# Second-half operand sums pinned over gate/up units 4 to 14, the last chunk's norm moved into unit 2, and the down stage's pools laid elsewhere

## The chip, the cores and the metric

The kernel runs on one core of a Trainium2 chip. The metric is device time in microseconds for one execution of the whole program; lower is better. The core has five engines with queues of their own that run in order: TensorE (PE), VectorE (DVE), ScalarE (ACT), GpSimd (POOL) and SyncE (SP), which here issues nearly all of the loads and stores. An instruction at the head of a queue that waits for a semaphore holds everything behind it on that queue.

## The reference

One transformer block on 2048 tokens of width 1024: three kinds of self-attention, a projection, cross-attention over 256 memory tokens, and a gated feed-forward layer. The change touches the seam between the cross-attention and the feed-forward layer, the feed-forward layer's first half, and the start of its down projection:

```python
def _rmsnorm(x, g):
    y = xf * lax.rsqrt(jnp.mean(xf * xf, axis=-1, keepdims=True) + EPS)
    return y * g
...
x = x + _cross(_rmsnorm(x, norm_cross), _rmsnorm(mem, norm_mem), w_cq, w_ckv, w_co)
h = _rmsnorm(x, norm_ffn)
gate, up = jnp.split(h @ w_gu, 2, axis=-1)          # 1024 -> 2 x 2816
x = x + (jax.nn.silu(gate) * up) @ w_down           # 2816 -> 1024
return _rmsnorm(x, final_norm)
```

## The kernel before, in words

All is fp32; each matmul operand is split into a rounded high part (`h`, a cast on ACT) and the rest (`l`, a subtraction on DVE or POOL), and a product is three matmuls (`mm3`, L87 to L95). Tokens lie in four chunks of 512 columns. A scheduler puts the instructions of each engine into an order of its own from the program's order and from the pools' tiles; an instruction that is given to `tc.keep_in_program_order` keeps its program place among those so pinned on its engine. Tiles of one tag share `bufs` buffers, and a new tile waits for the last use of the one that it replaces.

**Cross-attention** runs 16 units `u` (four heads for each chunk). `soft` (L1057) makes the probabilities `cp` of a unit, normalised by `l` at L1074; `turn_p` transposes them on PE (L1082); `outp` (L1098 to L1106) multiplies by `w_co`, adds the residual and adds squares into `ssum` on POOL (L919). `rows` (L1108 to L1115) transposes a chunk's result back to row order for a store. `norm1` and `norm2` (L1117 to L1134) give the feed-forward norm of a chunk: column sums on PE (`rc`, L925), a reciprocal root on ACT and DVE, a diagonal `dg`, a broadcast matmul, a copy `rb`, and eight scalings (L1132), whose results go to DRAM as `s_h3`. Chunks 0 and 1 form the first half of the feed-forward stage, chunks 2 and 3 the second.

**Gate and up** run two halves of 22 units `f`. A unit is a Strassen-like step: seven products p1, p5, p2, p6, p7, p3, p4 in this order, each 12 matmuls of 128x512, so 84 matmuls. The token-side operands of a half are "11", "t1", "21", "t2", "t3", "22", "t4", with four parts each; `turn1` (L1165 to L1168) splits a part, with part 3's low half on POOL and the others on DVE. The weight-side operands come from `prep_w(f)` (L1292 on): two loads `graw` (three buffers), sums s1 to s4 on DVE (L1304 to L1307), and seven splits `awh`, `awl` (L1239, L1240; four buffers; products 0, 3 and 6 on DVE, the rest on POOL). A unit's results are added on DVE, ACT and POOL and stored as `s_g` (L1372, L1382).

**The second half's sums.** `second(j)`, called before units 3, 7, 11 and 15, makes the operands of the second half from `s_h3` of chunks 2 and 3: four loads, three casts on ACT (L1257), three splits (L1258) and four subtractions (L1263 to L1268) on POOL, and nine stores to `s_b`. `refill` (L1272) loads them back near the first half's end. Nothing in it is pinned in this kernel.

**Down** (L1427 on) runs groups of two hidden blocks `js`, the first group of one. `weights` loads `draw` from `w_down` and makes sums; `tokens` loads `graw` from `s_g`; `parts` splits either (cast L1441, low part L1443) into `wdh`, `wdl`, `gdh`, `gdl`; the matmuls are at L1547. All of its pools lie on the left of the SBUF, the raw loads `draw` first, over the tiles of the gate and up stage that its last unit still stores from.

Of the kernel before, what the change touches and what calls it, by code (L numbers as in the profile page):

```python
# [33 lines left out]
def kernel(ctx: ExitStack, tc: tile.TileContext, a: dict, out: bass.AP, dbg=None):  # L34
# [9 lines left out]
    def scratch(shape, name):  # L44
        if name in dbg:
# [15 lines left out]
    s_x2 = [[scratch([P, CH], f"s_x2_{c}_{k}") for k in range(KT)] for c in range(NCH)]  # L61
    s_x3 = [scratch([CH, D], f"s_x3_{c}") for c in range(NCH)]
    s_b = {n: [[scratch([P, CH], f"s_b{n}_{j}_{i}") for i in range(2 if n in ("11", "t1", "21") else 1)]
               for j in range(4)] for n in ("11", "t1", "21", "t2", "t3", "t4")}
    s_h3 = [[scratch([P, CH], f"s_h3_{c}_{k}") for k in range(KT)] for c in range(NCH)]
# [855 lines left out]
    def rms_cols(st):  # L921

        ps = pp.tile([P, CH], F32, name="rc", tag="tp", bufs=2)
        for t in range(4):
            nc.tensor.matmul(ps[:, t:t + 1], st[0][:, t * P:(t + 1) * P], ones[:, 0:1], start=True, stop=True)  # L925
# [131 lines left out]
    def soft(u, q):  # L1057
# [15 lines left out]
        for t in range(4):  # L1073
            nc.vector.tensor_scalar_mul(pt[:, t, :], pt[:, t, :], l[:, t:t + 1])  # L1074
        return pt
# [62 lines left out]
    def load_wc(k):  # L1138
        th, tl = wp.tile([P, D], F32R, name=f"wch{k}"), wp.tile([P, D], F32R, name=f"wcl{k}")
        for n in range(2):  # L1140
            r = lp.tile([P, CH], F32, name="wraw", tag="x3", bufs=9)
            nc.sync.dma_start(r, a["w_co"][0][k * P:(k + 1) * P, n * 512:(n + 1) * 512])
            split(r, th[:, n * 512:(n + 1) * 512], tl[:, n * 512:(n + 1) * 512])
        wc.append((th, tl))
# [88 lines left out]
    with ExitStack() as es:  # L1233
# [11 lines left out]
        def turn(B, n, raw):  # L1245
            for j in range(4):
                turn1(B, n, j, raw[j])

        def second(j):

            b11, b21, b12, b22 = (pools["fx"].tile([P, CH], F32, name="ht", tag="ht", bufs=16) for _ in range(4))
            for x, y in zip((b11, b21, b12, b22), (s_h3[2][j], s_h3[2][4 + j], s_h3[3][j], s_h3[3][4 + j])):
                nc.sync.dma_start(x, y)

            def parts(n, x):
                t = [pools["fx"].tile([P, CH], F32, name="ht", tag="ht", bufs=16) for _ in range(2)]
                nc.scalar.copy(t[0].bitcast(F32R), x)  # L1257
                nc.gpsimd.tensor_sub(t[1].bitcast(F32R), x, t[0])  # L1258
                for i in range(2):
                    nc.sync.dma_start(s_b[n][j][i], t[i])  # L1260

            parts("11", b11)
            nc.gpsimd.tensor_sub(b11, b12, b11)  # L1263
            parts("t1", b11)
            nc.gpsimd.tensor_sub(b12, b22, b12)
            nc.gpsimd.tensor_sub(b11, b22, b11)
            parts("21", b21)
            nc.gpsimd.tensor_sub(b21, b21, b11)  # L1268
            for n, x in (("t2", b11), ("t3", b12), ("t4", b21)):
                nc.sync.dma_start(s_b[n][j][0], x)  # L1270

        def refill():  # L1272
# [126 lines left out]
        xlate.close()  # L1399
# [225 lines left out]
```

## Time and profile before

| | |
|---|---|
| three runs | 2868.70, 2869.55, 2871.01 us; median 2869.55 |
| the profiled execution | 2869.44 us, of which the span is 2867.7 |
| PE busy | 2734.8 us, 95% of the span |
| DVE, ACT, POOL busy | 1865.8 (65%), 1316.5 (46%), 1356.4 (47%) |
| DMA | 409.76 MB, mean 143 GB/s |

The span is what the profiler saw from the first to the last instruction. PE's share is so high that shares alone say little; what counts are the stretches in which PE stands still or runs at the lower of its two clock levels. PEclk in a view of stretches is the clock granted as a share of the full 2.4 GHz; 0.5 is 1.2 GHz. A wait is put down to the instruction that released it.

### The profile page before, as it was taken

How to read it: one execution, taken by the hardware profiler on the slowest of the kernel's cores; microseconds unless marked ns; L12 is line 12 of the kernel's file. 1: busy time of each engine (PE TensorE's matmuls, PEld its weight loads, DVE VectorE, ACT ScalarE, POOL GpSimd, SP SyncE). 2: the span in 40 equal slices, each digit the busy share in tenths (PEclk: the TensorE clock that was granted, in tenths of full speed). 3: DMA queues.
4: the chain of work that ended last, by engine and by line, in shares of the span. 5: the costliest groups of instructions: out<-in, count | busy, mean ns of one | idle time of the engine just before them, and what ended most of it. 6: DMA issues, size and time to landing. Idle time of an engine off the chain costs nothing. (4 is left out here: it accounts for less than half of the span.)

```text
span 2867.7 us, 40584 instructions
## 1 busy us (share of the span) xinstructions
PE 2734.8 (95%) x13409; PEld 2289.6 (80%) x13409; DVE 1865.8 (65%) x3560; ACT 1316.5 (46%) x2780; POOL 1356.4 (47%) x1069
## 2 busy tenths in 40 slices
PE   7999999999999979999997899999999996999996
PEld 7889888888888858878875688887888885788885
DVE  6446458887777774265576566667666665677778
ACT  5325119998776644244444333334333334433335
POOL 3232253332111121221257876666777665679754
PEclk9999999999999989999998899999999998999998
DMA  7755557433342254333355633335333334445434
GB/s 249 254 181 203 189 188 221 127 104 113 114 121 77 69 187 140 107 121 118 114 182 186 234 102 108 103 103 174 105 111 100 110 103 142 144 151 180 140 96 143
DMA packets 340130, 409.76 MB, mean 143 GB/s; under 512 B 43136, under 2 KB 194944, under 8 KB 339920
## 3 DMA queue, kind: packets, MB, share of 16 engines
q1 hardware_dynamic: 316944, 388.01, 42.1%
q10 hardware_dynamic: 22976, 19.16, 2.1%
q8 instruction: 106, 1.74, 0.3%
q14 instruction: 104, 0.85, 0.1%
HBM read 268.51 MB, written 138.56 MB: 142 GB/s over the span
## 5 line engine op out<-in xcount | busy, mean ns | idle before, releaser
L773 POOL TENSOR_TENSOR ptl<-pf,pth 128x512 fp32r<-128x512 f32 (+3 forms) x111 | 110.0, 991 | 360.5 <-ACT pth L772 244.3
L1554 DVE TENSOR_TENSOR acc<-dn,acc 128x512 f32<-128x512 f32 x352 | 225.4, 681 | 67.7 <-PE dn L1547 65.3
L1547 PE MATMUL dn<-wdh,gdh 128*128 128x512 f32 x616 | 238.2, 394 | 23.0 <-ACT gdh L1441 16.3
L1240 POOL TENSOR_TENSOR awl<-s,awh 128x512 fp32r<-128x512 f32 x132 | 205.6, 1558 | 104.1 <-ACT awh L1239 93.1
L1547 PE MATMUL dn<-wdl,gdh 128*128 128x512 f32 x616 | 241.8, 392 | 2.5 <-DVE wdl L1443 2.5
L1547 PE MATMUL dn<-wdh,gdl 128*128 128x512 f32 x616 | 236.3, 392 | 0.0
L1239 ACT CAST awh<-s 128x512 fp32r<-128x512 f32 x176 | 109.4, 622 | 247.5 <-PE mm L95 239.6
L724 ACT ACTIVATE pt<-pt,m 128x640 f32<-128x640 f32 (+4 forms) x192 | 205.4, 1074 | 31.6 <-DVE pt L710 29.7
L764 PE MATMUL tp<-ident,pt 128*128 128x128 f32 x1368 | 217.6, 273 | 1.2 <-ACT pt L724 1.2
L776 DVE TENSOR_TENSOR ptl<-tp,pth 128x512 fp32r<-128x512 f32 (+3 forms) x321 | 183.2, 587 | 47.4 <-ACT pth L775 45.9
L1441 ACT CAST gdh<-graw 128x512 fp32r<-128x512 f32 x154 | 95.1, 622 | 236.2 <-PE dn L1547 137.5
L919 POOL TENSOR_TENSOR ssum<-ssum,sq 128x512 f32<-128x512 f32 x56 | 73.3, 1309 | 264.1 <-ACT sq L918 245.4
L764 PEld LDWEIGHTS tp<-ident,pt 128*128 128x128 f32 x1368 | 165.7, 140 | 27.4 <-ACT pt L724 1.6
L775 ACT CAST pth<-tp 128x512 fp32r<-128x512 f32 (+3 forms) x321 | 159.1, 518 | 44.2 <-PE tp L764 40.0
L790 PE MATMUL pv<-ptl,va 128*128 128x512 f32 (+3 forms) x432 | 165.9, 390 | 0.0
L1443 POOL TENSOR_TENSOR gdl<-graw,gdh 128x512 fp32r<-128x512 f32 x94 | 132.5, 1420 | 70.5 <-ACT gdh L1441 46.7
L704 PE MATMUL s<-ka,qa 128*128 128x512 f32 (+8 forms) x432 | 163.2, 381 | 1.8 <-DVE r L562 0.6
L1239 ACT CAST awh<-graw 128x512 fp32r<-128x512 f32 x132 | 81.8, 620 | 177.9 <-PE mm L95 116.0
L790 PE MATMUL pv<-pth,va 128*128 128x512 f32 (+3 forms) x432 | 159.6, 372 | 0.4 <-ACT pth L775 0.4
L1547 PEld LDWEIGHTS dn<-wdh,gdh 128*128 128x128 f32 x616 | 116.4, 189 | 52.3 <-ACT gdh L1441 16.7
L1547 PEld LDWEIGHTS dn<-wdl,gdh 128*128 128x128 f32 x616 | 116.7, 189 | 26.9 <-DVE wdl L1443 2.9
L1547 PEld LDWEIGHTS dn<-wdh,gdl 128*128 128x128 f32 x616 | 116.8, 190 | 24.5
(436 smaller groups left out, 8404.6 us busy)
## 6 DMA issues: line engine op xcount, KB each, us to landing
graw<-in_w_gu_dram SPq DMA_DIRECT2D x88, 512.0 KB
graw<-s_g SPq DMA_DIRECT2D x154, 256.0 KB
s_g<-pair SPq DMA_DIRECT2D x66, 256.0 KB
x<-s_x SPq DMA_DIRECT2D x64, 256.0 KB
wr<-in_w_in_dram SPq DMA_DIRECT2D x48, 256.0 KB
s_g<-u SPq DMA_DIRECT2D x44, 256.0 KB
draw<-in_w_down_dram SPq DMA_DIRECT2D x22, 512.0 KB
ht<-s_h SPq DMA_DIRECT2D x36, 256.0 KB
```

The costliest lines, as they stand in the source:

```text
L704: nc.tensor.matmul(dst, l, r, start=j == 0, stop=j == len(seq) - 1)
L724: nc.scalar.activation(v.pt[:, 0:nk * P], v.pt[:, 0:nk * P], AF.Exp, bias=v.prev, scale=-1.0, accum_out=u.l[:, t:t + 1])
L764: nc.tensor.transpose(ps[:, t * P:(t + 1) * P], u.p[t][:, o:o + P], ident)
L773: nc.gpsimd.tensor_sub(lo[:, cs], pf[:, cs], f32(hi[:, cs]))
L775: nc.scalar.copy(hi[:, cs], ps[:, cs])
L776: nc.vector.tensor_sub(lo[:, cs], ps[:, cs], f32(hi[:, cs]))
L790: nc.tensor.matmul(st.ps[:, cs], l, r[:, cs], start=b == blocks[0] and j == 0, stop=b == blocks[-1] and j == len(seq) - 1)
L1239: nc.scalar.copy(tiles[0], raw)
L1240: (nc.gpsimd if k else nc.vector).tensor_sub(tiles[1], raw, f32(tiles[0]))
L1443: (nc.vector if cnt[0] % n == 0 else nc.gpsimd).tensor_sub(t[1], x, f32(t[0]))
L1547: nc.tensor.matmul(ps[t], l[:, ts], r, start=p == chain[0][0] and i == 0, stop=i == len(seq) - 1, skip_group_check=True)
L1554: nc.vector.tensor_add(x, ps[t], x)
```

## The change

- `soft(15)` normalises its four probability tiles on ACT instead of DVE.
- Chunk 3 is stored to `s_h3[3]` un-normalised, right after each `outp`. Its `ssum` goes through DRAM (`s_ss`); `last_norm`, in unit 2 of the first half, reads it back and makes `rb` with the same column sums, root, diagonal and broadcast as before. `norm1` and `norm2` of chunk 3 at the head of the stage go; two of its eight scalings are done in each `second(j)`, which also stores "22" to `s_b`.
- `second(j)` is now a list of loads and eight pieces of work. The loads stand ahead of units 3, 6, 9 and 12; four pieces run in each of units 4 and 5, 7 and 8, 10 and 11, 13 and 14, behind products p1, p2, p7 and p4. Its casts, splits, subtractions and scalings are pinned, as are the `rc` matmuls, the broadcast of `last_norm` and the casts of `load_wc`, which go from the helper `split` to the same two operations written out.
- The down stage's raw loads lie on the right of the SBUF, over `fx` (the raw operands, free early in the second half); the split tokens follow there. `fgain`, `ot`, the split weights and the sums `acc` lie on the left. In the first group only p = 3 loads its tokens into `ot`; before, p = 6 did too.

```diff
+    s_ss = scratch([P, CH], "s_ss")
...
-               for j in range(4)] for n in ("11", "t1", "21", "t2", "t3", "t4")}
+               for j in range(4)] for n in ("11", "t1", "21", "t2", "t3", "22", "t4")}
...
+    pin = tc.keep_in_program_order
...
-            nc.vector.tensor_scalar_mul(pt[:, t, :], pt[:, t, :], l[:, t:t + 1])
+            if u < 15:
+                nc.vector.tensor_scalar_mul(pt[:, t, :], pt[:, t, :], l[:, t:t + 1])
+            else:
+                nc.scalar.mul(pt[:, t, :], pt[:, t, :], l[:, t:t + 1])
...
+        def last_norm():
+
+            ss = pools["fx"].tile([P, CH], F32, name="ht", tag="ht", bufs=16)
+            nc.sync.dma_start(ss, s_ss)
+            rs, nt = rms_cols([ss])
+            nc.vector.tensor_mul(rs, rs, nt)
+            dg = pools["fx"].tile([P, CH], F32, name="ht", tag="ht", bufs=16)
...
+                pin(nc.tensor.matmul(ps[:, t * P:(t + 1) * P], ones, dg[:, t * P:(t + 1) * P], start=True, stop=True))
+            rb.append(pools["fx"].tile([P, CH], F32, name="rb"))
+            nc.scalar.copy(rb[0], ps)
...
+            def norm(x, k):
+                pin(nc.vector.scalar_tensor_tensor(out=x, in0=x, scalar=gains[:, G_FFN + k:G_FFN + k + 1], in1=rb[0],
+                                                   op0=ALU.mult, op1=ALU.mult))
...
-                nc.scalar.copy(t[0].bitcast(F32R), x)
-                nc.gpsimd.tensor_sub(t[1].bitcast(F32R), x, t[0])
+                pin(nc.scalar.copy(t[0].bitcast(F32R), x))
+                pin(nc.gpsimd.tensor_sub(t[1].bitcast(F32R), x, t[0]))
...
+            return loads, [norms, lambda: parts("11", b11), lambda: sub(b11, b12, b11), lambda: parts("t1", b11),
+                           lambda: sub(b12, b22, b12, "t3"), lambda: sub(b11, b22, b11, "t2"),
+                           lambda: parts("21", b21), lambda: sub(b21, b21, b11, "t4")]
...
             outp(3, oT, m, x3, st)
+            nc.sync.dma_start(s_h3[3][m], x3[m])
...
+        nc.sync.dma_start(s_ss, st[0])
         begun = [w0, acc(), acc()]
         block(begun[1], w0[0], B["11"])
+        block(begun[2], w0[1], B["t1"])
         rows(3, 7, x3)
-        dg = norm1(st)
-        block(begun[2], w0[1], B["t1"])
-        norm2(3, x3, dg)
...
-                if half == 0 and f in (3, 7, 11, 15):
-                    second((f - 3) // 4)
+                if half == 0 and f == 2:
+                    last_norm()
+                if half == 0 and f in (3, 6, 9, 12):
+                    loads, work = second(f // 3 - 1)
+                    loads()
+                elif half == 0 and 3 < f < 15:
+                    after = {p: work.pop(0) for p in ("p1", "p2", "p7", "p4")}
...
-        rp = pool(es, "dr")
+        rp = pool(es, "dr", side="right")
+        gp = pool(es, "dg", side="right")
+        xp = pool(es, "dx")
         wp = pool(es, "dw")
-        gp = pool(es, "dg")
-        xp = pool(es, "dx")
+        accp = pool(es, "da")
...
-                if len(js) == 1 and p in (6, 3):
+                if len(js) == 1 and p == 3:
```

How the order moves, at three places. The first is POOL from the last products of the seam into unit 1. `b..._3l` is the low half of a part 3 of unit 0's operands, L1405 (L1442 in the changed kernel) makes the operand t4, `awl` is a weight split, `pair` and `z5` are sums of a unit, and L1258 to L1265 belong to `second`. Before:

```order
L1168 TENSOR_TENSOR b21_3l_17951<-ht_17397,b21_3h_17950 128x512
L1405 TENSOR_TENSOR ht_17395<-ht_17395,ht_17387 128x512
L1168 TENSOR_TENSOR bt2_3l_17967<-ht_17389,bt2_3h_17966 128x512
L1405 TENSOR_TENSOR ht_17397<-ht_17397,ht_17389 128x512
L1168 TENSOR_TENSOR bt3_3l_18001<-ht_17405,bt3_3h_18000 128x512
L1168 TENSOR_TENSOR b22_3l_18032<-ht_17413,b22_3h_18031 128x512
L1258 TENSOR_TENSOR ht_18422<-ht_18413,ht_18421 128x512
L1168 TENSOR_TENSOR bt4_3l_18068<-ht_17397,bt4_3h_18067 128x512
L1263 TENSOR_TENSOR ht_18413<-ht_18415,ht_18413 128x512
L1351 TENSOR_TENSOR pair_17970<-u2_18035,z5_17972 128x512
L1240 TENSOR_TENSOR awl_18122<-s1_18109,awh_18121 128x512
L1265 TENSOR_TENSOR ht_18415<-ht_18416,ht_18415 128x512
```

The same stretch of POOL in the changed kernel:

```order
L1176 TENSOR_TENSOR b21_3l_17921<-ht_17402,b21_3h_17920 128x512
L1442 TENSOR_TENSOR ht_17400<-ht_17400,ht_17392 128x512
L1176 TENSOR_TENSOR bt2_3l_17937<-ht_17394,bt2_3h_17936 128x512
L1442 TENSOR_TENSOR ht_17402<-ht_17402,ht_17394 128x512
L1176 TENSOR_TENSOR bt3_3l_17971<-ht_17410,bt3_3h_17970 128x512
L1176 TENSOR_TENSOR b22_3l_18002<-ht_17418,b22_3h_18001 128x512
L1176 TENSOR_TENSOR bt4_3l_18038<-ht_17402,bt4_3h_18037 128x512
L1388 TENSOR_TENSOR pair_17940<-u2_18005,z5_17942 128x512
L1248 TENSOR_TENSOR awl_18092<-s1_18079,awh_18091 128x512
L1393 TENSOR_TENSOR z5_17942<-z5_17942,u2_18005 128x512
L1248 TENSOR_TENSOR awl_18096<-graw_18075,awh_18095 128x512
```

The rows of `second` (L1258, L1263, L1265) have left the queue here, one of them from between the splits of "22" and "t4"; the seven rows of unit 0's own operands stand in their old order.

The second place is POOL in unit 4, where it splits weights of unit 5 already (in the changed kernel L1291 and L1296 are the splits and subtractions of `second`, L1388 to L1399 the sums of a unit, L1248 the weight splits). Before:

```order
L1380 TENSOR_TENSOR pair_18304<-g1_18529,u2_18545 128x512
L1240 TENSOR_TENSOR awl_18638<-s4_18612,awh_18637 128x512
L1351 TENSOR_TENSOR pair_18645<-u2_18704,z5_18647 128x512
L1240 TENSOR_TENSOR awl_18771<-s1_18758,awh_18770 128x512
L1356 TENSOR_TENSOR z5_18647<-z5_18647,u2_18704 128x512
L1240 TENSOR_TENSOR awl_18775<-graw_18754,awh_18774 128x512
L1362 TENSOR_TENSOR pair_18645<-pair_18645,z5_18647 128x512
```

POOL at the same place in the changed kernel:

```order
L1248 TENSOR_TENSOR awl_18613<-s4_18587,awh_18612 128x512
L1291 TENSOR_TENSOR ht_18668<-ht_18413,ht_18667 128x512
L1388 TENSOR_TENSOR pair_18620<-u2_18688,z5_18622 128x512
L1296 TENSOR_TENSOR ht_18413<-ht_18415,ht_18413 128x512
L1248 TENSOR_TENSOR awl_18762<-s1_18749,awh_18761 128x512
L1393 TENSOR_TENSOR z5_18622<-z5_18622,u2_18688 128x512
L1248 TENSOR_TENSOR awl_18766<-graw_18745,awh_18765 128x512
L1399 TENSOR_TENSOR pair_18620<-pair_18620,z5_18622 128x512
L1291 TENSOR_TENSOR ht_18737<-ht_18413,ht_18736 128x512
L1248 TENSOR_TENSOR awl_18774<-s3_18751,awh_18773 128x512
L1248 TENSOR_TENSOR awl_18778<-s4_18752,awh_18777 128x512
L1296 TENSOR_TENSOR ht_18415<-ht_18416,ht_18415 128x512
```

Four rows of `second(0)` stand here between the weight splits and the sums, where there were none.

The third place is ACT at the seam of gate/up and down. `u4` is the last activation of gate/up, `wdh` a cast of down weights (`draw`, or a sum `t2`, `t3`), `gdh` a cast of tokens. Before:

```order
L1361 ACTIVATE u4_24950<-u4_24950 128x512
L1441 CAST wdh_25056<-draw_25047 128x512
L1441 CAST gdh_25070<-graw_25068 128x512
L1441 CAST gdh_25076<-graw_25074 128x512
L1441 CAST gdh_25082<-graw_25080 128x512
L1441 CAST gdh_25152<-graw_25150 128x512
```

ACT at the same seam in the changed kernel:

```order
L1398 ACTIVATE u4_24962<-u4_24962 128x512
L1485 CAST gdh_25085<-graw_25083 128x512
L1485 CAST gdh_25091<-graw_25089 128x512
L1485 CAST gdh_25097<-graw_25095 128x512
L1485 CAST gdh_25167<-graw_25165 128x512
L1485 CAST wdh_25071<-draw_25062 128x512
L1485 CAST wdh_25075<-t2_25067 128x512
L1485 CAST wdh_25079<-t3_25066 128x512
L1485 CAST wdh_25157<-draw_25062 128x512
L1485 CAST wdh_25161<-draw_25063 128x512
L1485 CAST wdh_25213<-draw_25063 128x512
```

Four casts of tokens now stand ahead of the first cast of weights, and all six weight casts follow one another. The loads of the first `draw` tiles, which on SP came behind the last stores of `s_g`, now come about 130 rows earlier on SP.

## Rows read from the trace of the kernel before

**Rows 1.** Stretches: window, us, busy (instructions) by engine, PEclk, DMA share, GB/s.
```profile
1463.50:1474.00 10.50, 5.64 (x17) 3.97 (x17) 10.50 (x11) 2.97 (x7) 9.88 (x8) 0.67 0.22 67
1497.70:1541.50 43.80, 30.25 (x127) 23.28 (x126) 27.64 (x42) 23.05 (x42) 29.45 (x17) 0.81 0.40 131
1541.50:1623.70 82.20, 64.58 (x248) 50.57 (x247) 44.39 (x41) 25.86 (x45) 79.33 (x57) 0.85 0.73 247
1705.30:1743.38 38.08, 38.08 (x169) 31.54 (x168) 23.66 (x27) 13.08 (x22) 26.35 (x19) 1.00 0.32 104
1568.00:1610.00 42.00, 29.73 (x111) 23.52 (x110) 20.98 (x18) 12.24 (x22) 41.98 (x30) 0.80 0.77 261
2393.00:2440.00 47.00, 25.33 (x89) 19.18 (x89) 33.83 (x38) 23.77 (x46) 28.34 (x20) 0.78 0.67 221
```

**Rows 2.** PE's waits from 1455 to 1640: us in total, times, longest.
```profile
PE mm L95 <- DVE u L1349: 7.6, 1, 7.6
PE tp L1082 <- DVE cp L1074: 4.9, 4, 2.4
PE mm L95 <- ACT z L1338: 4.7, 1, 4.7
PE mm L95 <- DVE b_0l L1168: 4.7, 1, 4.7
PE mm L95 <- DVE g L1343: 4.5, 1, 4.5
PE mm L95 <- POOL b_3l L1168: 3.4, 2, 2.9
PE tp L1128 <- DVE dg L1122: 2.5, 1, 2.5
```

**Rows 3.** Timeline of DVE: start, us, line, out<-in, count, [idle before <- releaser].
```profile
1464.38 5.25 DVE L1074 TENSOR_SCALAR cp<-cp,cl 128x256 f32<-128x256 f32 x4
...
1513.55 5.39 DVE L1132 SCALAR_TENSOR_TENSOR x<-x,gains,rb 128x512 f32<-128x512 f32 x8 [2.32 <-ACT rb L1130]
1518.86 0.68 DVE L1168 TENSOR_TENSOR b_0l<-ht,b_0h 128x512 fp32r<-128x512 f32 x1
...
1598.49 0.96 DVE L1304 TENSOR_TENSOR s<-graw 128x512 f32<-128x512 f32 x1 [5.70 <-DMA graw<-in_w_gu_dram]
```

**Rows 4.** Timeline of POOL, 1519 to 1594.
```profile
1519.62 8.91 POOL L1405 TENSOR_TENSOR ht<-ht 128x512 f32<-128x512 f32 x2 [13.26 <-DVE b_0l L1168]
1528.49 1.27 POOL L1168 TENSOR_TENSOR b_3l<-ht,b_3h 128x512 fp32r<-128x512 f32 x1
...
1539.01 1.73 POOL L1168 TENSOR_TENSOR bt_3l<-ht,bt_3h 128x512 fp32r<-128x512 f32 x1
...
1592.19 1.73 POOL L1240 TENSOR_TENSOR awl<-graw,awh 128x512 fp32r<-128x512 f32 x1
```

**Rows 5.** Timeline of ACT, 1508 to 1591.
```profile
1508.84 0.59 ACT L1114 COPY xs<-tp 128x512 f32<-128x512 f32 x1
...
1534.64 1.28 ACT L1344 ACT_TABLE_LOAD   x1
...
1590.38 0.62 ACT L1257 CAST ht<-ht 128x512 fp32r<-128x512 f32 x1 [4.88 <-DMA ht<-s_h]
```

**Rows 6.** PE's waits from 2385 to 2460.
```profile
PE dn L1547 <- ACT gdh L1441: 16.3, 1, 16.3
PE dn L1547 <- ACT acc L1552: 4.4, 2, 2.8
PE dn L1547 <- DVE wdl L1443: 2.5, 1, 2.5
```

**Rows 7.** Timeline of SP's queue, 1593 to 2404.
```profile
1593.95 0.38 SPq L1296 DMA_DIRECT2D graw<-in_w_gu_dram  x1
...
2397.53 0.55 SPq L1382 DMA_DIRECT2D s_g<-pair  x1
2403.47 0.81 SPq L1453 DMA_DIRECT2D draw<-in_w_down_dram  x2
```

**Rows 8.** Timeline of ACT, 2407.
```profile
2407.17 0.62 ACT L1441 CAST wdh<-draw 128x512 fp32r<-128x512 f32 x1 [15.05 <-DMA draw<-in_w_down_dram]
```

More of the change, by code (lines that the diff above doesn't have):

```diff
@@ L924, in rms_cols @@
         for t in range(4):
-            nc.tensor.matmul(ps[:, t:t + 1], st[0][:, t * P:(t + 1) * P], ones[:, 0:1], start=True, stop=True)
+            pin(nc.tensor.matmul(ps[:, t:t + 1], st[0][:, t * P:(t + 1) * P], ones[:, 0:1], start=True, stop=True))
         ss = sp.tile([P, 4], F32, name="rms_ss", tag="rms_ss", bufs=4)
@@ L1142, in load_wc @@
             nc.sync.dma_start(r, a["w_co"][0][k * P:(k + 1) * P, n * 512:(n + 1) * 512])
-            split(r, th[:, n * 512:(n + 1) * 512], tl[:, n * 512:(n + 1) * 512])
+            ns = slice(n * 512, (n + 1) * 512)
+            pin(nc.vector.tensor_copy(th[:, ns], r))
+            nc.gpsimd.tensor_sub(tl[:, ns], r, f32(th[:, ns]))
         wc.append((th, tl))
@@ L1247, in turn @@
                 turn1(B, n, j, raw[j])
-        def second(j):
-            b11, b21, b12, b22 = (pools["fx"].tile([P, CH], F32, name="ht", tag="ht", bufs=16) for _ in range(4))
-            for x, y in zip((b11, b21, b12, b22), (s_h3[2][j], s_h3[2][4 + j], s_h3[3][j], s_h3[3][4 + j])):
-                nc.sync.dma_start(x, y)
+        rb = []
+        def last_norm():
[4 more added lines that the diff above has]
+            dg = pools["fx"].tile([P, CH], F32, name="ht", tag="ht", bufs=16)
+            for t in range(4):
+                nc.vector.tensor_scalar(out=dg[:, t * P:(t + 1) * P], in0=ident, scalar1=rs[:, t:t + 1], scalar2=None,
+                                        op0=ALU.mult)
+            ps = pp.tile([P, CH], F32, name="tp", tag="tp", bufs=2)
+            for t in range(4):
+                pin(nc.tensor.matmul(ps[:, t * P:(t + 1) * P], ones, dg[:, t * P:(t + 1) * P], start=True, stop=True))
+            rb.append(pools["fx"].tile([P, CH], F32, name="rb"))
+            nc.scalar.copy(rb[0], ps)
@@ new lines, in second, with loads @@
+        def second(j):
+            b11, b21, b12, b22 = x = [pools["fx"].tile([P, CH], F32, name="ht", tag="ht", bufs=16) for _ in range(4)]
+            def loads():
+                for x, y in zip((b11, b21, b12, b22), (s_h3[2][j], s_h3[2][4 + j], s_h3[3][j], s_h3[3][4 + j])):
+                    nc.sync.dma_start(x, y)
+            def norm(x, k):
+                pin(nc.vector.scalar_tensor_tensor(out=x, in0=x, scalar=gains[:, G_FFN + k:G_FFN + k + 1], in1=rb[0],
+                                                   op0=ALU.mult, op1=ALU.mult))
@@ L1255, in parts @@
             def parts(n, x):
                 t = [pools["fx"].tile([P, CH], F32, name="ht", tag="ht", bufs=16) for _ in range(2)]
-                nc.scalar.copy(t[0].bitcast(F32R), x)
-                nc.gpsimd.tensor_sub(t[1].bitcast(F32R), x, t[0])
+                pin(nc.scalar.copy(t[0].bitcast(F32R), x))
+                pin(nc.gpsimd.tensor_sub(t[1].bitcast(F32R), x, t[0]))
                 for i in range(2):
                     nc.sync.dma_start(s_b[n][j][i], t[i])
-            parts("11", b11)
@@ L1263, in second, with sub @@
[L1263 to L1270, printed above, removed]
+            def sub(o, x, y, n=None):
+                pin(nc.gpsimd.tensor_sub(o, x, y))
+                if n:
+                    nc.sync.dma_start(s_b[n][j][0], o)
@@ L1272, in refill, with norms @@
+            def norms():
+                norm(b12, j)
+                norm(b22, 4 + j)
+                nc.sync.dma_start(s_b["22"][j][0], b22)
+            return loads, [norms, lambda: parts("11", b11), lambda: sub(b11, b12, b11), lambda: parts("t1", b11),
+                           lambda: sub(b12, b22, b12, "t3"), lambda: sub(b11, b22, b11, "t2"),
+                           lambda: parts("21", b21), lambda: sub(b21, b21, b11, "t4")]
         def refill():
@@ L1278, in refill @@
                 for j in range(4):
-                    nc.sync.dma_start(raw[n][j], s_h3[3][4 + j] if n == "22" else s_b[n][j][0])
+                    nc.sync.dma_start(raw[n][j], s_b[n][j][0])
             def direct(n):
@@ L1427 @@
     with ExitStack() as es:
-        rp = pool(es, "dr")
+        rp = pool(es, "dr", side="right")
+        gp = pool(es, "dg", side="right")
+        xp = pool(es, "dx")
         wp = pool(es, "dw")
-        gp = pool(es, "dg")
-        xp = pool(es, "dx")
+        accp = pool(es, "da")
         pp = pool(es, "dpp", space=PSUM)
         fgain = xp.tile([P, D], F32, name="fgain")
-        acc = [xp.tile([P, D], F32, name=f"acc{t}") for t in range(16)]
+        acc = [accp.tile([P, D], F32, name=f"acc{t}") for t in range(16)]
         lo, hi = slice(0, 512), slice(512, 1024)
```

## The prediction

> **What bounds the kernel now.** I read the stretches first, then PE's waits, then the queues of the engines that PE waits for. In a steady stretch of gate/up PE is never idle and two units take 38.08 us [rows 1], so 168 matmuls come at 0.2267 us each and a unit takes 19.04. Nothing in such a stretch can be won on another engine. What can be won lies at two seams. Units 1 to 3 of the first half are 252 matmuls, 57.1 us at that pace, and took 82.2 us (1541.5 to 1623.7; a few matmul records are missing there): a loss of 25.1 us. Ahead of that, unit 0 starts on waits: PE's list from 1455 to 1640 shows 4.9 us for the probabilities `cp`, 2.5 for the diagonal `dg`, 4.7 for `b_0l` and 3.4 for `b_3l` [rows 2]. At the start of down the list shows 16.3, 4.4 and 2.5 us [rows 6]. The granted clock is 0.81, 0.85 and 0.78 of full in these stretches and 1.00 in the steady one [rows 1], so after a long wait matmuls run at 1.2 GHz for a time. In units 1 to 3 the three long waits make 16.8 us [rows 2], small ones under 2, and the rest of the 25.1, some 7 us, is the low clock: about 2.4 us behind each long wait. I use that as the price of a long wait's clock.
>
> **Probabilities of unit 15.** DVE took 5.25 us for the four scalings [rows 3], 1.3 each, and PE's transposes waited for them one by one. In the changed kernel they stand on ACT behind a short root, ahead of its other work; ACT was busy 2.97 of 10.5 us around there [rows 1]. No row shows this operation on ACT. A 128x512 copy, twice as wide, takes 0.59 [rows 5], so four take at most 2.4 us, and the last tile is ready by about 1466.2 instead of 1469.6: 3.4 us, and more as the first comes earlier too. The ceiling is the 4.9 us of the wait and a us of clock. I take 4.5 (3 to 6).
>
> **Last norm put off.** Before, DVE made `dg`, waited, and did eight scalings from 1513.55 for 5.39 us; only then came `b_0l`, at 1518.86 [rows 3], and POOL, which begins with sums that wait for it, at 1519.62 [rows 4]. With norm and scalings gone, ACT's casts follow the last copy `xs`, which ended at 1509.4 [rows 5] and stays (its buffers wait for stores); a cast of 0.6 later DVE can split, at about 1510. Everything behind moves up by 8.8 us: the end of `b_3l` from 1529.8 to 1521.0, and that of the last split, "t4", from 1540.7 to 1530.2, as one POOL row of 1.75 us between leaves as well [rows 4]. The 2.9 us wait for `b_3l` (within the 3.4) moves along, it does not go. I take 9 us (6, if ACT is held by the stores longer, to 11). The s_h3 stores of chunk 3 now go out without waiting for the norm; the load of `s_ss` waits on SP for POOL's first sum, near 1515, and behind it stand the weight loads of unit 2. Those could not go out then anyway: their buffer is freed by unit 0's last weight split, later than 1520. Price: nothing, and if that cover is gone, some us of a load in a unit that starts over 30 us later.
>
> The norm comes back in unit 2. Its column sums and broadcast are moved, not added. Three table loads on ACT are new, at 1.28 us [rows 5]. Between sums and broadcast lie three products, 36 matmuls or 8.2 us. The chain through ACT and DVE cost PE 2.5 us of waiting before [rows 2] with little work beside it; two table loads lie in it, 2.6 us, and it queues behind other work on both engines. 5 to 10 us against a cover of 8.2: I take 1 us (0 to 4).
>
> **Units 0 to 3 without `second`.** POOL was busy 41.98 of 42 us from 1568 to 1610 [rows 1]. Its row at 1592.19 is a weight split that ended at 1593.92 [rows 4]; it frees a `graw` buffer, and SP issued the next load at 1593.95 [rows 7]; DVE stood 5.70 us for that load at 1598.49 [rows 3], in front of sums that PE needed. So the 7.6 us wait is POOL's queue, handed on through the loads. The 4.7 us wait for `z` is ACT's: it stood 4.88 us at 1590.38 with a cast of `second` whose load had not landed, the copy `z` behind it [rows 5]. Both causes are gone: by the order none of `second`'s work is in these units. What is late next is the load itself: in unit 1 the next weights' load can go out only when POOL has split the third weight, I estimate near 1535, and must land before DVE's sums, near 1540; PE needs what is queued behind them at about 1549. So it fits with several us. I take 21 of the 25.1 us; from 10 (the first of the three waits and half of another stay) to 25.
>
> **Units 4 to 14.** Each `second(j)` gives POOL seven operations in two units. POOL's mean in the steady stretch is 26.35/19 = 1.39 us, so 4.9 us a unit on 13.2: 18.1 of 19.04, with every third unit free of it. ACT (6.5 of 19 busy) and DVE (11.8) have room for three casts and two scalings [rows 1]. DMA gets 14 transfers of 256 KB in 38 us, some 96 GB/s on 104; stretches with 247 and 261 GB/s are in the same rows. The cover is the four weight buffers, some three products or 8 us. Steady rows show no stall, so I take 2 us in all; from nothing to the rivals below.
>
> **Start of down.** Before, the last `s_g` store went out at 2397.53, the first `draw` load waited for it until 2403.47 [rows 7], its cast ran at 2407.17 [rows 8], and PE stood 16.3 us from 2393.4. In the changed kernel `draw` is loaded and its sums are made within the second half. Four token casts now stand ahead on ACT; three of their loads also come early, the fourth goes out behind DVE's first token split, near 2395.4 by its 0.7 us steps, and needs between 3.7 us (2403.47 to 2407.17) and 5.9 us (the store above). With two casts behind it the first matmul comes at 2400.5 to 2402.7: a wait of 7 to 9 us, 8 less. The six weight splits follow one another, so the 2.5 us go; of the 4.4 us for `acc` I take 2, as its copies no longer queue behind those casts. Waits of 23.2 us and 89 matmuls at 0.2267, 20.2 us, leave 3.6 of the 47 us to the clock [rows 1]; 1.5 goes. Together 14 (7 to 18).
>
> **The sum.** 4.5 + 9 + 21 + 14 - 1 - 2 = 45.5 us. The profiled execution took 2869.4, 0.1 under the median, so no correction: 2823.9, say 2824.
>
> **Rivals.** (a) The new work holds a queue as in unit 3 before: a pinned cast or split of `second` stands at the head of ACT or POOL with its input not ready, a weight split behind it. Price per hold: 4.7 us and 2.4 of clock. Once for each j, 28 us: 2852. For it: ACT's row at 1590.38. Against it: loads now go out a unit ahead. (b) Down is held by the late token load or by DVE's splits, and gains 3 instead of 14: 2835. For it: four casts now stand ahead of the weights in order. (c) Weights still come late in units 1 to 3, gain 10 instead of 21: 2835. For it: DVE's order still has the sums ahead of what PE needs.
>
> (d) Slower: POOL does not fit. Place: units 4 to 14. Two of its operations took 8.91 us beside DVE's back-to-back splits [rows 4], 4.46 each. At that price the 3.5 new ones make 15.6 on 13.2, 28.8 us in a unit of 19.04; eight such units lose 78: 2902. It decides from 3.4 us each, where eight units lose the 45.5. Against it: the mean was 41.98/30 = 1.40 even with POOL full [rows 1], as DVE is busy 62% in such units, not throughout. The Trainium skill, "SBUF — State Buffer", "Who interferes with whom", says that a VectorE instruction with two SBUF inputs contends with a GpSimd instruction that reads SBUF, which speaks for this rival; the 8.91 us row agrees with it, the steady stretch only at a small part of that price. (e) Scheduler and waits undo it: the time stays. The order speaks against it.
>
> **How the numbers follow.** Forecast 0.55 (its own range 2812 to 2838), (a) 0.09, (b) 0.14, (c) 0.12, (d) 0.07, (e) 0.03. Low end: all upper bounds and no cost, 6 + 11 + 25 + 18 = 60: 2809. High end: all lower bounds, 26, and 6 of cost: 2849, say 2850. Outside lie (a), (d) and (e), 0.19. About 0.2% is what a measurement of this kernel can tell from no change. Faster by more: 0.90; within: 0.03, (e); slower: 0.07, (d).
>
> **What would show it.** Right: `b_0l` on DVE some 9 us after the last `ssum` work and no scalings ahead of it, PE gaps over 4 us gone from units 1 to 3, units 4 to 14 at 19.04 us each, PE's wait at the start of down 7 to 9 us. Wrong: POOL busy throughout units 4 to 14 with PE waiting for `awl` there; a PE wait at the broadcast in unit 2; `gdh` or `wdl` ahead of PE's first down matmul by more than 9 us.

## The result, and the profile after

The changed kernel takes 2853.91 us (median of four runs, 2849.23 to 2854.26) against 2870.28 for the kernel before beside it: a ratio of 0.9938, 95% interval 0.9921 to 0.9955. It is faster, as forecast, but by some 17 us and not 45; the time lies 4 us above the range. The profiled execution took 2853.96 us, its span 2852.2, which is 15.5 under that of before. Four runs of one kernel differ by up to 5 us here, so sizes below come from places in the traces, and whole times only for what is larger.

The same PE instruction can be looked up in both traces. How far PE was ahead of the kernel before at some places, in us, and what the prediction had for the stretch up to there:

| stretch, up to | ahead at its end | change in it | predicted |
|---|---|---|---|
| cross-attention ahead of unit 15 (its column sums at 1461.28, now 1457.76) | 3.5 | -3.5 | 0 |
| unit 15, to the first gate/up matmul (1497.73, now 1495.85) | 1.9 | +1.6 | -4.5 |
| unit 0 (84 matmuls on, 1540.33, now 1532.95) | 7.4 | -5.5 | -9 |
| units 1 to 3 (unit 4 starts at 1593.65, was 1623.71) | 30.1 | -22.7 | -20 |
| units 4 to 21 of the first half | 17.7 | +12.4 | +2 |
| second half of gate/up | 18.3 | -0.6 | 0 |
| first matmul of down (2409.77, now 2381.14) | 28.6 | -10.3 | -14 |
| end of down | 15.5 | +13.1 | 0 |

Two stretches gave back 25 us: the units in which the second half's sums now run (8.7 us by the end of unit 14, 3.7 in unit 15), and, unforeseen, the whole of down after its start. Stretches of the changed kernel (window, us, busy and count by engine, granted clock, DMA share, GB/s):

```profile
1593.65:1957.50 363.85, 357.22 (x1551) 290.60 (x1549) 249.81 (x253) 130.24 (x231) 286.95 (x196) 1.00 0.49 166
...
2375.00:2422.00 47.00, 36.76 (x133) 27.11 (x132) 31.59 (x44) 29.79 (x58) 28.39 (x21) 0.89 0.63 211
...
2440.00:2790.00 350.00, 350.00 (x1496) 281.35 (x1495) 245.41 (x360) 112.60 (x205) 246.38 (x167) 1.00 0.42 134
```

The first row is units 4 to 21 and some three products after them: 1551 matmuls at 0.2267 us are 351.6, so 12.2 us are lost. The second answers to the last of [rows 1]: 133 matmuls instead of 89 in 47 us. The third is down in full flow, and it is the surprise. PE is busy throughout at the full clock and yet makes 1496 matmuls in 350 us, 0.2340 us each. In the kernel before, 350 us of the same stage hold 1543, 0.2268 each:

```profile
2460.00:2810.00 350.00, 349.84 (x1543) 289.35 (x1543) 259.53 (x381) 118.73 (x216) 258.16 (x175) 1.00 0.46 141
```

0.0072 us more for each of 1848 matmuls are 13.3 us. No wait shows it; the busy share of PE even rose to 96%. PE's waits of the changed kernel, from 1455 to 1600 (answering to [rows 2]):

```profile
PE mm L98 <- ACT b_0h L1175: 5.1, 1, 5.1
PE tp L1134 <- DVE pl L164: 3.5, 1, 3.5
PE mm L98 <- DVE bt_2l L1176: 1.5, 2, 0.7
PE tp L1271 <- DVE ht L1267: 1.5, 1, 1.5
```

and from 2370 to 2430 (answering to [rows 6]), with ACT's queue there (answering to [rows 8]):

```profile
PE dn L1591 <- ACT wdh L1485: 6.0, 1, 6.0
PE dn L1591 <- ACT acc L1596: 5.8, 4, 2.9
```

```profile
2379.95 0.62 ACT L1485 CAST gdh<-graw 128x512 fp32r<-128x512 f32 x1 [4.62 <-DMA graw<-s_g]
2380.47 0.61 ACT L1485 CAST wdh<-draw 128x512 fp32r<-128x512 f32 x1
```

The three long waits of units 1 to 3 are gone; what is left there is the wait at the broadcast of the norm that was put off, 1.5 us; unit 2 as a whole takes 2.8 us more than 19.04. Down starts 6.0 us after gate/up, behind the late token load that the prediction named.

### The profile page after: what moved, and what is told of

Read it like the earlier page. It is cut to its first block, busy times and chain, and to the rows that moved or that the text cites. A ratio compares the mean times of both kernels' runs of the same rounds, so it can differ in the third digit from the quotient of the medians.

```text
span 2852.2 us, 40541 instructions
## 1 busy us (share of the span) xinstructions
PE 2745.8 (96%) x13409; PEld 2285.0 (80%) x13409; DVE 1858.6 (65%) x3556; ACT 1315.6 (46%) x2787; POOL 1353.7 (47%) x1069
## 5 line engine op out<-in xcount | busy, mean ns | idle before, releaser
L1248 POOL TENSOR_TENSOR awl<-s,awh 128x512 fp32r<-128x512 f32 x132 | 203.1, 1540 | 68.3 <-ACT awh L1247 68.3
L767 PEld LDWEIGHTS tp<-ident,pt 128*128 128x128 f32 x1368 | 165.7, 140 | 27.2 <-ACT pt L727 1.4
L1591 PEld LDWEIGHTS dn<-wdh,gdl 128*128 128x128 f32 x616 | 117.4, 191 | 28.6
```

The source lines that it names most:

```text
L767: nc.tensor.transpose(ps[:, t * P:(t + 1) * P], u.p[t][:, o:o + P], ident)
L1248: (nc.gpsimd if k else nc.vector).tensor_sub(tiles[1], raw, f32(tiles[0]))
L1591: nc.tensor.matmul(ps[t], l[:, ts], r, start=p == chain[0][0] and i == 0, stop=i == len(seq) - 1, skip_group_check=True)
```

## Experiments

Labels of kernels are those of the headings. All whose name does not begin with "before" are the changed kernel with an edit. Ratios are to the kernel before in the same session.

### The pace in down

In the built program the split tokens `gdh` and `gdl`, the stationary operand, start at 157664 and every 2048 bytes on, 96 over a multiple of 128; the split weights `wdh` and `wdl`, the moving operand, at 34688, a multiple of 128. Before, both started at multiples of 128. The gate/up stage on the same side of the SBUF begins with an unused tile of 96 bytes, the new pools of down do not. Theory A: these addresses set the pace. Rival B: it is the place of the sums, or traffic.

**pad24**

```diff
         rp = pool(es, "dr", side="right")
+        rp.tile([P, 24], F32, name="pad")
```

> The changed kernel with one unused tile of 96 bytes at the start of the down stage's raw-load pool on the right. It moves the split tokens gdh and gdl, the stationary operand of down's matmuls, from addresses of 32 over a multiple of 64 to multiples of 64; nothing else moves. Theory A (address of the stationary operand sets the pace): 0.2340 us a matmul between 2440 and 2790 goes back to 0.2268, 1848 matmuls gain 12 to 14 us, 2853.9 becomes 2840 to 2842. Rival B (the pace comes from where acc or the weights lie now, or from traffic): the pace stays at 0.2340 and the time at 2854.

**pad8**: the same line with 8 for 24.

> The same with 32 bytes: tokens at 64 over a multiple of 128. Theory A with a step of 64 bytes: 0.2268 us a matmul, as with 96. With a step of 128 bytes: 0.2340. Rival B: 0.2340.

**before_tok32** (the kernel before; a tile of 32 bytes at the start of `dg`, and one at the start of `dx`):

```diff
         gp = pool(es, "dg")
+        gp.tile([P, 8], F32, name="offg")
         xp = pool(es, "dx")
+        xp.tile([P, 8], F32, name="offx")
```

> The kernel before with gdh and gdl moved by 32 bytes; all else in down stays at multiples of 64. Theory A: pace in down 0.2268 to 0.2340, 12 to 14 us more than 2869. Rival B: pace stays 0.2268, time 2869.

**before_w32**: the two tiles at the start of `dw` and of `dg` instead, so weights at 32 and tokens at 64.

> The kernel before with the split weights wdh and wdl, the moving operand of down's matmuls, moved by 32 bytes, the tokens at a multiple of 64. If the address counts for the stationary operand only: pace 0.2268, time 2869. If for either operand: 0.2340 or more, 12 us more at least.

**before_wonly32**: `dg` laid ahead of `dw`, the tiles at the start of `dw` and `dx`: tokens at 0, weights at 32.

> The kernel before with the pools of split tokens and split weights changed in order, so that gdh and gdl start at a multiple of 128 bytes and wdh and wdl, the moving operand, 32 bytes over one. If the moving operand's address counts by itself: pace in down about 0.2333 us. If only the stationary operand's counts (the slow pace of before_w32 was then its tokens, at 64 over a multiple of 128): 0.2267.

**before_both32**: the tiles at the start of `dw` and `dx`, the order of the pools as before: weights and tokens both at 32.

> The kernel before with tokens and weights both 32 bytes over a multiple of 128. If the pace hangs on the two addresses' difference: 0.2267. If on each operand's own address: 0.2333 or slower.

Measured, 350 us of down in each. pad24:

```profile
2440.00:2790.00 350.00, 348.61 (x1538) 288.39 (x1537) 256.17 (x380) 118.12 (x217) 254.87 (x173) 1.00 0.46 139
```

pad8:

```profile
2440.00:2790.00 350.00, 349.63 (x1499) 280.74 (x1498) 248.75 (x360) 113.35 (x204) 247.36 (x168) 1.00 0.44 134
```

before_tok32, before_wonly32 and before_both32, in this order:

```profile
2460.00:2810.00 350.00, 350.00 (x1501) 282.00 (x1500) 250.12 (x358) 110.51 (x195) 251.78 (x170) 1.00 0.44 136
```

```profile
2460.00:2810.00 350.00, 349.50 (x1499) 280.42 (x1498) 251.60 (x357) 108.05 (x188) 250.95 (x170) 1.00 0.45 136
```

```profile
2460.00:2810.00 350.00, 349.86 (x1544) 289.38 (x1543) 258.55 (x382) 118.02 (x218) 257.92 (x174) 1.00 0.47 141
```

Busy time over count:

| kernel | tokens, weights over a multiple of 128 | us per matmul |
|---|---|---|
| before | 0, 0 | 0.2267 |
| changed | 96, 0 | 0.2340 |
| pad24 | 0, 0 | 0.2267 |
| pad8 | 64, 0 | 0.2332 |
| before_tok32 | 32, 0 | 0.2332 |
| before_w32 (1502 in 350) | 64, 32 | 0.2330 |
| before_wonly32 | 0, 32 | 0.2332 |
| before_both32 | 32, 32 | 0.2266 |

The same sign stands in the profile of before, in cross-attention. There the stationary operand of the query projection, `wqh` and `wql`, starts 96 over a multiple of 128 in the built program and the moving one, `fth` and `ftl`, at a multiple. In the multiplication by `w_co` beside it both lie alike. From 1300 to 1448 (count: least, median and longest time in ns):

```profile
L95 PE MATMUL mm<-ol,wch x74: 387/389/431, 1300.2 to 1438.4; 128*128 128x512 f32 x74
L95 PE MATMUL mm<-fth,wqh x71: 390/397/499, 1310.7 to 1447.6; 128*128 128x512 f32 x71
```

Nine of the query projection in a row, from 1296.52 to 1298.63, come 0.234 us apart; 21 by `w_co`, from 1302.49 to 1307.25, come 0.2267 apart.

Theory A holds in the form that before_both32 leaves: not either operand's own address, but the difference of the two. Every difference in the remainder by 128 that was tried, 32, 64 and 96 bytes, costs 0.0063 to 0.0073 us of 0.2267, about 3%. In all the quick cases the two addresses differ by whole multiples of 512 bytes, so the runs do not tell whether 128 or 256 would do as well. In whole times: pad24 took 2846.07 us (ratio 0.9902, interval 0.9886 to 0.9919), pad8 2854.4, before_tok32 2879.2, before_w32 and before_wonly32 2882.0 each, before_both32 2867.9, with the kernel before at 2873.2 and 2872.6 in those sessions. All but pad24 are single runs. By the ratios pad24 gains 10 us over the changed kernel (0.9938 less 0.9902), where 12 to 14 were expected. What in the chip does it stays open; the runs show the remainder, not a mechanism.

**old_pools** (the changed kernel with before's pools and token tiles in down):

```diff
-        rp = pool(es, "dr", side="right")
-        gp = pool(es, "dg", side="right")
-        xp = pool(es, "dx")
-        wp = pool(es, "dw")
-        accp = pool(es, "da")
+        rp = pool(es, "dr")
+        wp = pool(es, "dw")
+        gp = pool(es, "dg")
+        xp = accp = pool(es, "dx")
...
-                if len(js) == 1 and p == 3:
+                if len(js) == 1 and p in (6, 3):
```

> The changed kernel with the down stage's pools and token tiles as before (all on the left, at multiples of 128 bytes). The new layout's worth alone: PE's waits at the start of down go back from 6.0 + 2.9 + 2.1 us to 16.3 + 2.5 + 2.8 + 1.6 or so, 10 to 12 us with the clock; the pace in down is 0.2268. Theory A then gives a time within 3 us of the changed kernel's 2853.9 on the same chip, as the layout won at the seam what it lost in the stage. If the 0.2340 comes from elsewhere, it would stay and the time be near 2865.

It took 2855.66 us, as the changed kernel within the spread, with PE's waits from 2370 to 2440 back:

```profile
PE dn L1590 <- ACT gdh L1484: 17.0, 1, 17.0
PE dn L1590 <- ACT acc L1595: 3.9, 4, 1.9
PE dn L1590 <- DVE wdl L1486: 2.8, 1, 2.8
```

Its matmuls in down come 0.227 us apart again. So the new layout by itself was worth nothing: what it won at the start of down, the remainder took back over the stage. With the 96 bytes it is worth some 13 us, by the ratios (0.9902 in pad24, 2855.66 over 2871.02 here, from one run).

### Units 4 to 14

The loss is 12.4 us, not all of it in units 4 to 14. By the starts of successive units, 3.5 us are lost in units 8 and 9, 4.1 in 10 to 12, and 4.7 in 14 and 15 (3.7 of these in unit 15). A chain that begins with the last sums of unit 7 and makes PE wait in unit 9 shows one way. POOL, SP, DVE and ACT of the changed kernel (start, us, what, and idle time before it with its releaser):

```profile
1683.98 2.99 POOL L1296 TENSOR_TENSOR ht<-ht 128x512 f32<-128x512 f32 x2
1686.93 1.73 POOL L1417 TENSOR_TENSOR pair<-g,u 128x512 f32<-128x512 f32 x1
```

```profile
1688.69 0.34 SPq L1419 DMA_DIRECT2D s_g<-pair  x1
```

```profile
1693.08 0.69 DVE L1380 TENSOR_TENSOR pair<-mm,p 128x512 f32<-128x512 f32 x1 [3.26 <-DMA s_g<-pair]
```

```profile
1693.86 0.63 ACT L1381 ACTIVATE pair<-pair 128x512 f32<-128x512 f32 x1 [9.64 <-DVE pair L1380]
1694.39 0.60 ACT L1290 CAST ht<-ht 128x512 fp32r<-128x512 f32 x1
1694.90 0.62 ACT L1247 CAST awh<-graw 128x512 fp32r<-128x512 f32 x1
```

```profile
1697.64 0.50 PE L98 MATMUL mm<-b_0h,awl 128*128 128x512 f32 x1 [1.34 <-POOL awl L1248]
```

Two subtractions of `second` ran ahead of the unit's last sum into `pair`, which has one buffer. Its store went out 3 us later for them and landed 4.4 us after that; DVE's next sum into `pair` waited for it, ACT's activation for DVE, and the casts behind it, one of them a weight cast, for ACT. POOL itself stood idle in between. The same rows come again behind unit 13 (subtractions at 1805.80, ACT idle for 9.88 us), and PE waits in unit 15. Theory C: POOL's work ahead of the splits and of `pair` makes the loss; C1, this chain alone; rivals, the casts, or the transfers.

**subs_dve**

```diff
-                pin(nc.gpsimd.tensor_sub(o, x, y))
+                pin(nc.vector.tensor_sub(o, x, y))
```

(with pad24's line, as in all that follow)

> The kernel with the 96-byte tile, and the four subtractions of each second(j) on DVE instead of POOL (three splits stay on POOL). Units 4 to 14 lost 12.3 us against 11 times 19.04 in the changed kernel. Theory C (the work that POOL got there stands ahead of weight splits and of the sums into pair): POOL loses 16 operations of 1.3 to 1.75 us, and 6 to 11 of the 12.3 us come back. Rival D (the loss comes from the casts on ACT or from the loads and stores of second, which stay): under 3 us come back.

**p4late**

```diff
-                    after = {p: work.pop(0) for p in ("p1", "p2", "p7", "p4")}
+                    after = {p: work.pop(0) for p in ("p1", "p2", "p7", "end")}
...
                 nc.sync.dma_start(dst[0], g1)
+                after.get("end", lambda: None)()
                 return
...
             eng.tensor_sub(a11, g1, u2)
+            after.get("end", lambda: None)()
```

> The kernel with the 96-byte tile, and the fourth piece of work in each of units 4 to 14 moved behind the unit's own sums in the program. In the changed kernel two subtractions (2.99 us) stand ahead of the last sum into pair in units 7 and 13; its store lands late, DVE waits 3.26 us for it, ACT's activation 9.6 us behind that with a weight cast behind it. Theory C1 (this chain makes the loss): the waits of 1.3 to 1.5 us in the units that follow go, 3 to 6 us come back. Rival C2 (POOL's amount of work, wherever it stands): under 2 us.

**no_pieces**

```diff
-                t = [pools["fx"].tile([P, CH], F32, name="ht", tag="ht", bufs=16) for _ in range(2)]
-                pin(nc.scalar.copy(t[0].bitcast(F32R), x))
-                pin(nc.gpsimd.tensor_sub(t[1].bitcast(F32R), x, t[0]))
                 for i in range(2):
-                    nc.sync.dma_start(s_b[n][j][i], t[i])
+                    nc.sync.dma_start(s_b[n][j][i], x)
...
-                pin(nc.gpsimd.tensor_sub(o, x, y))
```

> The kernel with the 96-byte tile and without the casts, splits and subtractions of second: its stores write the raw tiles instead, so the second half's operands are not those of the reference. Loads, stores and the two scalings stay. It is the floor for units 4 to 14: if theory C or the casts on ACT are the cause, the loss of 12.3 us is under 1 us; if the transfers are, it stays over 6.

The same 1551 matmuls as in the changed kernel's first row above, in p4late, subs_dve and no_pieces:

```profile
1593.40:1951.80 358.40, 353.75 (x1551) 291.76 (x1550) 248.83 (x253) 132.03 (x231) 287.03 (x196) 1.00 0.50 168
```

```profile
1593.90:1947.35 353.45, 352.41 (x1551) 290.53 (x1549) 250.96 (x269) 131.65 (x231) 267.51 (x180) 1.00 0.51 171
```

```profile
1595.40:1946.92 351.52, 351.52 (x1551) 290.81 (x1549) 230.77 (x253) 128.07 (x219) 244.78 (x169) 1.00 0.44 144
```

363.85 us in the changed kernel, 358.4, 353.45 and 351.5 here. Without the casts, splits and subtractions nothing is lost, so the transfers are innocent; with the four subtractions on DVE 10.4 of the 12.3 us come back, so the casts and the three splits, which stay there, leave 1.9 at most. p4late gains 5.5 us: in units 8 to 11, 14 and 15 nothing is lost any more, so the chain is gone, but units 6 and 12 now lose 1.7 and 5.2, with two waits for POOL's `awl` (4.6 us, one of 3.3). So the place of the work decides, and the place that was tried is only half of the cure. In whole times subs_dve took 2835.35 us (ratio 0.9877, 0.9860 to 0.9893), p4late 2838.67 (0.9890, 0.9875 to 0.9905), no_pieces 2834.79.

### Unit 15 and the head

**s15_dve** (on subs_dve):

```diff
-            if u < 15:
+            if u < 16:
```

> The kernel with the 96-byte tile and the subtractions on DVE, and unit 15's probabilities normalised on DVE as before. In the changed kernel the transposes of cp ended earlier but from the last of them to the first gate/up matmul it took 32.7 us against 27.1, as PE stood 3.5 us at the broadcast of chunk 2's norm. Theory E (PE-bound afterwards, the gain was given back there): from the start of unit 15 to the first gate/up matmul the time falls by 0 to 2 us with the scaling on DVE, and the whole time is within 2 us of the kernel on ACT. The prediction's step would have it 4.5 us slower.

**norm1_late** (on subs_dve):

```diff
-        if h == 3 and c:
+        if h == 3 and 0 < c < 3:
             dg = norm1(st)
...
     pts = turn_p(ppt)
+    dg = norm1(st)
     norm2(2, x3, dg)
```

> The kernel with the 96-byte tile and the subtractions on DVE, unit 15's probabilities on ACT, and norm1 of chunk 2 called behind turn_p of unit 15 in the program, so that DVE's two splits pl stand ahead of the root and the diagonal dg. Theory E1 (the gain of unit 15 on ACT was given back because DVE ran root and dg, 8.2 us, ahead of the splits that PE waited for): from the last transposition of cp to the first gate/up matmul it takes 27 to 29 us instead of 31.5, PE's 3.5 us wait at the broadcast goes, and the whole is 3 to 5 us faster than the kernel with the subtractions on DVE. Rival E2 (PE is held there by the broadcast of the norm whatever the order): 31 us or more, no gain.

DVE in the changed kernel, and then in s15_dve:

```profile
1468.02 3.92 DVE L1128 TENSOR_SCALAR dg<-ident,rms_rs 128x128 f32<-128x128 f32 x4
1471.86 1.27 DVE L164 TENSOR_TENSOR pl<-tp,ph 128x512 fp32r<-128x512 f32 x2
1475.32 5.39 DVE L1138 SCALAR_TENSOR_TENSOR x<-x,gains,rb 128x512 f32<-128x512 f32 x8 [2.19 <-ACT rb L1136]
```

```profile
1459.22 5.25 DVE L1078 TENSOR_SCALAR cp<-cp,cl 128x256 f32<-128x256 f32 x4
...
1470.18 0.68 DVE L164 TENSOR_TENSOR pl<-tp,ph 128x512 fp32r<-128x512 f32 x1
...
1472.79 0.87 DVE L1128 TENSOR_SCALAR dg<-ident,rms_rs 128x128 f32<-128x128 f32 x4
...
1475.01 5.39 DVE L1138 SCALAR_TENSOR_TENSOR x<-x,gains,rb 128x512 f32<-128x512 f32 x8 [0.43 <-ACT rb L1136]
```

ACT did its part: the last transposition of `cp` started at 1463.2, 7.4 us before that of the kernel before, 3.5 of them from earlier. But with the scalings gone the scheduler put root and `dg` ahead of the two splits `pl`, the four small `dg` operations took 3.92 us there instead of 0.87, and PE stood 3.5 us for `pl`. DVE reached chunk 2's scalings at 1475.3 with the scaling on ACT and at 1475.0 without. s15_dve took 2832.18 us (0.9863, 0.9847 to 0.9880); from the last transposition to the first gate/up matmul 27.2 us instead of 31.5. From the column sums ahead of unit 15 (1457.51, and 1458.79 in subs_dve) to that matmul it is 34.9 us instead of 36.6: the scaling on ACT costs 1.7 us there, as theory E had it. norm1_late removes the 3.5 us wait, and gains nothing: 2832.76 us (0.9856, 0.9840 to 0.9873), 33.6 us for the same stretch, as PE then waited for DVE's residual sums (2.0 us at 1490.7). So E1 names the wait, but not a gain, and E2 is nearer. That points to DVE as what bounds this seam; no run gives DVE less to do there. Among these three the whole times don't differ clearly.

**norm_head** (on subs_dve: `norm1`, `norm2` of chunk 3 at the head, no `last_norm`, no scalings in `second`)

```diff
-            nc.sync.dma_start(s_h3[3][m], x3[m])
...
-        nc.sync.dma_start(s_ss, st[0])
...
-        block(begun[2], w0[1], B["t1"])
         rows(3, 7, x3)
+        dg = norm1(st)
+        block(begun[2], w0[1], B["t1"])
+        norm2(3, x3, dg)
...
-                if half == 0 and f == 2:
-                    last_norm()
...
-                norm(b12, j)
-                norm(b22, 4 + j)
```

> The kernel with the 96-byte tile and the subtractions on DVE, and chunk 3's norm at the head of gate/up again (column sums, diagonal, broadcast, eight scalings; no last_norm, no scalings in second). By the prediction's step unit 0 starts its third product 8 to 9 us later, and unit 2 loses the 1.5 us wait at the broadcast: 7 to 8 us slower. Rival: the store of chunk 3's rows holds ACT as long without the norm, 3 us or less.

PE's waits from 1500 to 1600 in norm_head:

```profile
PE mm L98 <- DVE b_0l L1176: 4.7, 1, 4.7
PE mm L98 <- POOL b_3l L1176: 3.6, 1, 3.6
PE rc L928 <- ACT xs L1120: 2.0, 1, 2.0
PE tp L1134 <- DVE dg L1128: 2.0, 1, 2.0
```

PE's lag behind subs_dve was 1.8 us at the first gate/up matmul (3.1 ahead of unit 15; its wait at chunk 2's broadcast is 0.8 us instead of 3.5). It grew to 11.3 in unit 0's third product, 9.5 more, as the step had it. By unit 1 it was 8.2, by unit 2 7.4, and behind unit 2's broadcast 4.6, as the column sums, the broadcast and the wait there are gone. So 2.8 of the 9.5 stay. The whole took 2834.11 us (0.9868, 0.9853 to 0.9883), no slower than subs_dve by this measure; 2.8 us lie within the spread.

**wc_unpinned** (on subs_dve)

```diff
-            ns = slice(n * 512, (n + 1) * 512)
-            pin(nc.vector.tensor_copy(th[:, ns], r))
-            nc.gpsimd.tensor_sub(tl[:, ns], r, f32(th[:, ns]))
+            split(r, th[:, n * 512:(n + 1) * 512], tl[:, n * 512:(n + 1) * 512])
```

> The kernel with the 96-byte tile and the subtractions on DVE, and load_wc's casts unpinned as before. In the changed kernel PE gained 3.7 us between 1225 and 1241, at the first units of cross-attention, which the prediction put at nothing. Theory F (the pinned casts do that): PE is 3 to 4 us later there again, waits of 2.6 and 2.5 us at the first column sums and scores are back. Rival: another part of the change shifts the scheduler there, and the waits stay at 1.5 and 0.4 us.

PE's waits from 1225 to 1262 in the changed kernel, and in wc_unpinned to 1266:

```profile
PE mm L98 <- ACT ph L163: 1.5, 1, 1.5
PE rc L928 <- POOL ssum L922: 1.5, 1, 1.5
PE mm L98 <- ACT qh L163: 0.4, 1, 0.4
```

```profile
PE rc L928 <- POOL ssum L922: 3.0, 1, 3.0
PE mm L98 <- DVE cp L1071: 2.1, 1, 2.1
PE mm L98 <- ACT qh L163: 0.6, 1, 0.6
```

The pinned casts do win the two waits, as theory F says: PE in wc_unpinned is 0.7 us ahead of subs_dve at 1221 and 3.9 behind at 1241, 4.6 in all. Their place is taken in part by a new wait of 1.5 us for `ph`; by unit 15 wc_unpinned is 1.2 behind, so 1.9 of the 4.6 are left. The whole was 2833.72 us, in the spread of subs_dve.

## Why the prediction failed

- **Down was priced only at its start.** The step "start of down" looked at who waits for whom, and the sum took the stage behind it as unchanged. That step failed: the pools were moved to the right without the 96 bytes that keep the tokens' remainder equal to the weights', and all 1848 matmuls became 3% slower, 13 us. No wait in the profile of before could show it. But the pace was there to be read: 397 ns for a matmul of the query projection against 389 beside it, its operands' addresses differing by 96 bytes over a multiple of 512. The unused tiles of 96 bytes at the start of the other right-hand pools were a sign as well.
- **Start of down, 14 predicted, 10.3 seen at its first matmul.** The 16.3 us wait became 6.0 (7 to 9 forecast) and the wait for `wdl` went. The waits for `acc` did not fall from 4.4 to 2.4 but rose to 5.8: the term that was mis-sized.
- **Units 4 to 14, 2 predicted, 8.7 seen there and 3.7 in unit 15.** Rival (a) has the right kind, a queue held behind an operation whose input is late, but at 1 to 4 us a unit rather than 7 a hold. That its 2852 lies so near the measured time is luck: the 28 us that it puts here were 12.4, and most of the rest of the miss is down's pace. Rival (d), POOL full, is refuted: it was busy 287 of 364 us. (Its threshold, by its own terms, is 3.3 us and not 3.4.) The step took the four weight buffers as 8 us of cover and counted POOL's time; it did not follow the sum into `pair`, whose single buffer ties the next unit's first sum to a store's landing, and through DVE and ACT to the weight casts.
- **Unit 15, 4.5 predicted, 1.6 lost.** ACT's scalings were as quick as forecast, four in 1.7 us. What was late next is DVE, whose order the removal changed; the step named no such thing.
- **Last norm, 9 predicted, 5.5 seen at the end of unit 0.** `b_0l` began at 1510.35 on DVE, 8.5 us earlier and 8.8 predicted, so the step held where it was made; but 1.9 of that PE had already. The wait for `b_3l`, which was to move along, went, and waits for `bt_1l`, `bt_2l` and `b_1l`, 2.9 us, came. What the step missed besides is that most of it is returned later: norm_head shows 2.8 us left of it by unit 3.
- **Units 1 to 3, 20 predicted, 22.7 seen**, broadcast included. POOL's crowd was the cause, and the weights' loads were in time.
- **The start of cross-attention**, put at nothing, gave 3.7 us by 1241 and 3.5 ahead of unit 15. The pinned casts explain 1.9 of it there; the rest is open.
- **Signs of being wrong.** Two of those named came, PE waiting for `awl` in units 9, 11, 12 and 15 and at the broadcast of unit 2. None pointed at the pace in down.

The rule of the Trainium skill that was weighed, "SBUF — State Buffer", "Who interferes with whom", shows itself once more in the changed kernel, in another form. In unit 0 POOL and DVE now split side by side:

```profile
1511.12 3.36 POOL L1442 TENSOR_TENSOR ht<-ht 128x512 f32<-128x512 f32 x2 [7.29 <-DVE b_0l L1176]
```

```profile
1513.25 1.77 DVE L1176 TENSOR_TENSOR bt_0l<-ht,bt_0h 128x512 fp32r<-128x512 f32 x1
```

Before, the same work took POOL 8.91 us for two and DVE 0.68 each [rows 3, 4]; now POOL takes 3.36 and DVE 1.77. The trace agrees that the two contend; the price 4.46 that rival (d) used belongs to one arrangement. In units 4 to 15 none of POOL's new operations took more than 1.75 us.

## What to carry to other kernels

When tiles that feed matmuls move, compare the addresses of the stationary and the moving operand: differences of whole multiples of 512 bytes kept 0.2267 us a matmul here, and 32, 64 or 96 bytes more cost 3% over the whole stage without one visible wait. Work that is pinned between an engine's own steps should be followed to each single-buffered tile that the unit reuses, not only to the engine's busy share. The best versions run here, 96 bytes of padding and the subtractions on DVE, took 2832 to 2835 us, 1.2 to 1.4% under the kernel before; most of it comes from units 1 to 3 and the start of down.

## What was not expected of the hardware

- The pace of a 128x512 matmul with a 128x128 stationary operand, both fp32 from SBUF: 0.2267 us when the two start addresses differ by whole multiples of 512 bytes, 0.2330 to 0.2340 with 32, 64 or 96 bytes more or less, whichever operand was moved; PE counts as busy all the while and the granted clock is 1.00.
- Four `dg` scalings of 128x128 took 3.92 us on DVE in one order and 0.87 in another; why stays open.
